# A second group of seven products in the last output projection of a two-layer decoder trunk

## The chip, the cores and the metric

One core of a Trainium2 chip runs the whole program in one launch. The metric is the device time of one execution in microseconds (us); lower is better. Engine names follow the profile: PE (TensorE matmul), PEld (its weight loads), DVE (VectorE), ACT (ScalarE), POOL (GpSimd), SP (SyncE, here only a queue that issues transfers).

## The reference, cut to what matters

Two layers work on 256 tokens of width 2048 in float32. Each layer normalises x, projects it, runs three token mixers a, b and c, projects each mixer's output to 2048 columns, and merges and projects once more:

```
g = jax.nn.sigmoid(gates).reshape(b, s, N_BRANCH, D_MODEL)
merged = g[:, :, 0] * y_a + g[:, :, 1] * y_b + g[:, :, 2] * y_c
return x + merged @ w_out
```

After the second layer a last RMSNorm gives the output. The change concerns `merged @ w_out` (256 x 2048 by 2048 x 2048) of the second layer and the order of the work just before it.

## The kernel before, in words

**Three products for one.** A float32 product is made of three on PE: every operand is split in a high part (a cast) and a low part (the rest), and high*high, low*high and high*low are summed in PSUM. The activations are split once. Weights stream from DRAM in blocks of 128 x 1024 words (512 KB); each block is cast on ACT (`high`, L296) and its rest taken on DVE (`low`, L300) just before use. There are three buffers each for the two parts.

**Steps.** `run` goes through a list of steps. A *plain* step has one weight block (256 rows by 512 columns): 12 matmuls of 128 x 512, for two token tiles, two row tiles and three products. In iteration s, `run` asks for the raw block of step s + 7, splits the block of step s + 2, and issues the matmuls of step s. Events hang on steps: work that is issued at a fixed distance from a step. The engines take their instructions in the order in which they were issued, so the list is the planner here, and each event's offset is a due time.

**Seven.** The class `Seven` is Winograd's form of Strassen's scheme on 1024 rows by 1024 columns (8 row tiles, two column blocks): products M1 to M7, two half steps each (`M1a`, `M1b`) of 6 matmuls, so 84 matmuls, where eight plain steps have 96. A half step still needs one whole block split. M1, M2 and M3 take raw blocks. The other four take sums of blocks, which are made in two pieces of memory for each half, `homes` and `third`: `two` and `three` load them on SP's queue, `first_sums` and `second_sum` add on DVE, and `first_adds` and `last_sum` add by transfers on POOL's queue that accumulate in memory. M5 and M3 take sums of activations (`osums`, made by `output_sums` from the merged tiles of column blocks 0 and 1). Results lie in four PSUM banks X, Y, Z, W; after M6 and M7 DVE forks a bank (L627: Z, then W). `lead` says how many steps before M5 the homes are asked for; `adds` says which sums are transfers.

**How the merged tile reaches the projection.** `merged` (called one step after the last product of column block j of branch b) multiplies and adds on DVE (L1612, L1613), and `turned` transposes: DVE transposes in blocks of 32 (L340), four POOL transfers write to DRAM (L343), one reads back (L349, `back`). Then `use_m` splits the result into `mx[j]`: a cast on ACT (L713), the rest on DVE (L714). `turned` puts its two later stages in a list of pending work: `back` at two plain steps' worth of work after the merge, `use_m` at `later` of them (`LATER` is 10). One entry is worked on at a time, in order. Both are issued `behind()`, that is, behind the splits of the step two ahead. `mx[2]` and `mx[3]` feed the second half of the rows of the output projection.

**The order before, last layer.** Gates `h1` (a group of seven and eight plain steps `c`, `d`) run beside `y1[0:8]`; then come `y1[8:16]` alone, four plain steps of output columns q = 2, then the group `o` (columns q = 0 and 1) interleaved with the four first steps of q = 3 and more of q = 2, then the last plain steps `c`, `e`, `f` (q = 2, 0, 1). The tail has the last four blocks of q = 3, the squares, the norm and the store. In the first layer the output projection already has two groups, `n` and `o` in the string `second`.

Of the kernel before, what the change touches and what calls it, by code (L numbers as in the profile page):

```python
# [11 lines left out]
ALU = mybir.AluOpType  # L12
# [77 lines left out]
def trunk(ctx: ExitStack, tc: tile.TileContext, x, w_in, xt, w_a, w_b, w_c, w_out,  # L90
# [115 lines left out]
    @contextmanager  # L206
    def in_turn():
        with tc.high_priority(offset=URGENT), issue_after(newest_parts[1].ins):
            yield
# [94 lines left out]
    def unit(*args, **kw):  # L304
        u = load_unit(*args, **kw)
        high(u)
        low(u)
        return u[1:]
# [42 lines left out]
    def turned(srcs, use, later=LATER, tmp=None, soon=False):  # L351


        n = len(srcs)
        if tmp is None:
            tmp = tp.tile([P, n * 512], F32, tag="zt", bufs=1, name=nm("zt"))
        c = srcs[0].shape[1]
        z = away([v.rearrange("p (k e) -> p k e", e=P) for v in srcs], tmp[:, :n * c], soon)

        def rest():  # L360
            y = tp.tile([P, n * 512], F32, tag="zy", bufs=1, name=nm("zy"))
            y = y[:, :n * c].rearrange("p (u k i) -> p u k i", u=n * 4, i=32)
            back(z, y)
            yield later - 2
            yield from use(y)

        pending.append([count[0] + 2, rest()])
# [115 lines left out]
    def once(make):  # L483
        kept = []

        def get():
            if not kept:
                kept.append(make())
            return kept[0]

        return get
# [8 lines left out]
    class Seven:  # L500


        def __init__(self, w, cols, act, sums, lead=7, own=None, adds=False, room=None, wide=False, copy_at=0):
# [29 lines left out]
            def three(h):  # L533
# [7 lines left out]
                with after_raw():  # L541
                    nc.sync.dma_start(third[h], block(1, 1, h))

            def first_adds(h):
                nc.gpsimd.dma_start(third[h], block(0, 1, h), accum_op=ALU.add)

            def first_sums(h):
                if own is not None:
                    with in_turn():
                        raw = self.steps["M1", h].raw  # L550
                        nc.vector.tensor_add(raw, raw, homes[h])
                    return
                with in_turn():
                    if adds in (1, 2, 4):
                        nc.vector.tensor_add(homes[h], homes[h], self.steps["M1", h].raw)
                        return
                    nc.vector.tensor_add(third[h], third[h], homes[h])
                    nc.vector.tensor_add(homes[h], homes[h], self.steps["M1", h].raw)

            def second_sum(h):  # L560
                if own is not None:
                    if adds:
                        nc.gpsimd.dma_start(homes[h], block(1, 1, h), accum_op=ALU.add)
                    with in_turn():
                        if not adds:
                            nc.vector.tensor_add(homes[h], homes[h], third[h])
                        nc.vector.tensor_add(third[h], third[h], self.steps["M1", h].raw)
                    return
                with in_turn():
                    nc.vector.tensor_add(homes[h], third[h], homes[h] if adds == 4 else self.steps["M1", h].raw)  # L570
                if adds == 4:
                    first_adds(h)

            def last_sum(h):
# [32 lines left out]
            for h in range(2):  # L607
                if lead:
                    st["M5", h].at(-PARTS - lead, partial(two, h), True)
                    st["M5", h].at(-PARTS - (lead + 1 if own is None else 3), partial(three, h), True)  # L610
                st["M1", h].at(-PARTS + (own is not None), partial(first_sums, h), True)
                if adds in (1, 2) and own is None:
                    st["M5", h].at(-PARTS - lead + 2, partial(first_adds, h), True)
                st["M5", h].at(-PARTS + 1, partial(second_sum, h), True)
                st["M2", h].at(-PARTS + 2, partial(last_sum, h), True)
            self.two, self.three = two, three
# [198 lines left out]
    for layer in range(DEPTH):  # L815
# [775 lines left out]
        def mg(j, t, mgs=mgs):  # L1591
            return mgs[j // 2][:, j % 2, t, :]
# [85 lines left out]
        def merged(b, j, y):  # L1678
            sg = held.pop((b, j), None)
            with in_turn() if b == 1 else nullcontext():  # L1680
                merge(b, j, y, sg)
            if b == 1:
                with in_turn():
                    turned([mg(j, t) for t in range(NT)], partial(use_m, j), LATER - 3 * (j in (1, 3) and not last), soon=True)

        kept_x, acc3 = {}, once(wide_accs)

        def output(q, banks, k0):
            if last and q == 3:
                return [plain(wo, k, q * 512, mx, acc3, k == 0, False) for k in range(0, KC, 2)]  # L1690

            def finished():
                xc = kept_x.pop(q)
                emit_x(xc, banks(), q, q * 512, list(range(NT)))
                store_x(xc, q * 512)

            def ask():
                kept_x[q] = residual(q * 512, 512)

            banks = once(banks or wide_accs)  # L1700
            steps = [plain(wo, k, q * 512, mx, banks, k == 0, k == KD - 2) for k in range(k0, KD, 2)]
            steps[-1].at(1, finished).at(-4, ask)
            return steps
# [52 lines left out]

        zg["M4", 1].at(1, partial(gate_summed, 0))
        zg["M3", 1].at(1, partial(gate_summed, 1))
        for i, st in enumerate((y1[2][3], f1[0]) if not last else y1[3][:2]):
            st.at(0, partial(output_sums, i * 2, i * 2 + 1))  # L1760
        if last:
            zd[3].at(0, lambda: nc.sync.dma_start(fwl[0], fnw.partition_broadcast(P)))
        if last:
            o = Seven(wo, (p0 * 512, p0 * 512 + 512), mx, osums, 10, None, 3)
            qs = {}
            for q in range(4):
                own = q in (p0, p0 + 1)
                banks = (lambda v: lambda: [o.bank(n) for n in v])("ZW" if q - p0 else "XY") if own else None
                qs[q] = output(q, banks, KC if own else 0)
        else:  # L1770
            c, d = 2 - p0, 3 - p0
            places = [once(lambda: slot().rearrange("p a b -> p (a b)")) for _ in range(2)]
            o = Seven(wo, (p0 * 512, p0 * 512 + 512), mx, osums, 10, None, 4, places, True)
            n = Seven(wo, (c * 512, d * 512), mx, osums, 9, None, 4, None, False, 5)
            qs = {q: output(q, lambda g=g, v=v: [g.bank(i) for i in v], KC)
                  for q, g, v in ((c, n, "XY"), (d, n, "ZW"), (p0, o, "XY"), (p0 + 1, o, "ZW"))}
# [14 lines left out]
        steps += gather(thin + rest, y=y2[10:], g=g1, c=c1, d=d1)  # L1791
        if last:
            steps += gather("y*2 " + begin.replace("M6a y", "M6a").replace("M2a y", "M2a") + rest, g=h1, y=y1[:8], c=e1, d=f1)
            steps += y1[8:]
        else:
            steps += gather("y*2 " + begin.replace("M6a y", "M6a").replace("M2a y", "M2a") +
                            "g.M3a c g.M3b c g.M4a c g.M4b c y*4", g=h1, y=y1[:12], c=e1)
# [10 lines left out]
        steps[at_norm].at(0, norm)  # L1808
        c, d = 2 - p0, 3 - p0
        if last:  # L1810
            steps += qs[c][:4] + gather(
                "g.M1a d g.M5a g.M1b d g.M5b d g.M6a d g.M6b c g.M2a c g.M2b g.M7a g.M7b g.M3a e g.M3b e g.M4a f g.M4b f c*2 e*2 f*2",
                g=o, c=qs[c][4:], d=qs[d], e=qs[p0], f=qs[p0 + 1])
        else:
            second = ("n.M1a h n.M1b h*3 y n.M5a y n.M5b y n.M6a n.M6b y n.M2a n.M2b n.M7a n.M7b "
                       "o.M1a c o.M1b d o.M5a c o.M5b d o.M6a n.M4a o.M6b n.M4b c*2 o.M2a d o.M2b o.M7a o.M7b n.M3a n.M3b d "
                       "o.M3a e o.M3b e o.M4a e o.M4b e f*4")
            steps += gather(second, n=n, o=o, y=y1[12:], h=f1, c=qs[c], d=qs[d], e=qs[p0], f=qs[p0 + 1])
# [15 lines left out]
            nc.vector.tensor_scalar(half, known, -0.5 / D, -0.5 * EPS, op0=ALU.mult, op1=ALU.add)  # L1834
            nc.vector.tensor_scalar(known, known, 1.0 / D, EPS, op0=ALU.mult, op1=ALU.add)

        c0, n = 1536, 512
        xc = residual(c0, n)

        head = acc3()  # L1840
        accs = [head[0], acc_tile()]
        nc.vector.tensor_add(xc[:, 1, :], head[1], xc[:, 1, :])
        oh, ol = ([slot(F32R).rearrange("p (k a) t -> p k (a t)", a=2) for _ in range(2)] for _ in range(2))
        for k0 in range(0, KC, 2):
            ks = slice(k0 % 4, k0 % 4 + 2)
            unit(w_out[layer], KC + k0, 2, [(c0, n)], dst=(oh[k0 // 4][:, ks, :], ol[k0 // 4][:, ks, :]))
        for t in range(NT):
            m, r, b = (small(1) for _ in range(3))
            kn, hf, ss = known[:, t:t + 1], half[:, t:t + 1], ssq[:, t, 3:4]
            if t < NT - 1:  # L1850
                for h in range(2):
                    token_products([accs[t]], n, (oh[h], ol[h]), mx, KC + h * 4, 4, KD, [t])
                emit_x(xc, [accs[t]], 3, c0, [t])
            else:

                token_products([accs[t]], n, (oh[0], ol[0]), mx, KC, 4, KD, [t], KC)
                token_products([accs[t]], n, (oh[1], ol[1]), mx, KC + 4, 2, KD - 2, [t], KC)
                with tc.high_priority(offset=URGENT):
                    nc.vector.tensor_add(xc[:, t, :], accs[t], xc[:, t, :])
                sa, kn, hf = (small(1) for _ in range(3))  # L1860
# [82 lines left out]
```

## Time and profile before

| what | value |
|---|---|
| three runs, median (lowest to highest) | 1976.4 us (1975.78 to 1977.06) |
| the profiled execution, its own time | 1976.76 us |
| its span, first to last instruction | 1974.7 us |
| PE busy | 1962.6 us (99%), 9158 matmuls |
| DVE busy | 1724.7 us (87%), 2022 instructions |
| ACT busy | 1357.5 us (69%), 1782 instructions |
| POOL busy | 234.2 us (12%), 354 instructions |
| granted TensorE clock, mean | 0.999 of full speed |

The span is what the instructions cover; the execution's own time has 2.06 us more around it. A busy share is an average over the whole span: an engine at 87% can be full for 20 us and half idle for the next 20.

### The profile page before, as it was taken

Reading aid. Unit: us, or ns where it says so; the run is one execution under the profiler, and the core shown is the slowest. Engines: PE = TensorE matmul, PEld = TensorE weight load, DVE = VectorE, ACT = ScalarE, POOL = GpSimd, SP = SyncE. Lnnn points to the kernel's source line nnn. Section 1 sums busy time; section 2 is a strip of 40 time slices with the busy share of each in tenths; the row PEclk is TensorE's granted clock in tenths of the full one; section 3 lists DMA queues with packets and bytes.
Section 4 is the critical chain, followed back from the end, with each engine's and each line's share of the span. In section 5 each row is a group of like instructions: output and inputs, shape, how many; then the busy total and the mean of one; then the engine's idle time right before and its main releaser. Section 6 shows DMA issues by size and latency. Waiting matters only on the chain.

```text
span 1974.7 us, 26272 instructions
## 1 busy us (share of the span) xinstructions
PE 1962.6 (99%) x9158; PEld 1642.7 (83%) x9158; DVE 1724.7 (87%) x2022; ACT 1357.5 (69%) x1782; POOL 234.2 (12%) x354
## 2 busy tenths in 40 slices
PE   9999999999999999999999999999999999999998
PEld 8888888888888888887888888888888888888886
DVE  8788999988998899889896988999889988898786
ACT  7567657679887666565665666676798876765654
POOL 0011102210100001012200211112101000011010
PEclk9999999999999999999999999999999999999999
DMA  7778759765888779889967787688659787798883
GB/s 276 279 253 270 238 188 315 266 226 190 257 265 268 235 243 297 268 288 322 331 232 277 250 270 233 199 294 280 218 180 290 246 285 249 242 294 270 288 279 136
DMA packets 147205, 507.86 MB, mean 257 GB/s; under 512 B 18368, under 2 KB 22976, under 8 KB 146944
## 3 DMA queue, kind: packets, MB, share of 16 engines
q1 hardware_dynamic: 116832, 409.18, 58.4%
q0 software_dynamic: 28576, 93.87, 19.0%
q10 hardware_dynamic: 1664, 3.15, 0.4%
q8 instruction: 71, 1.16, 0.2%
q14 instruction: 62, 0.51, 0.1%
HBM read 473.35 MB, written 32.77 MB: 256 GB/s over the span
## 4 chain that ended last, share of the span: by engine, by line
PE 98%; DVE 1%; issue 0%; DMA 0%; ACT 0%; DVEq 0%
PE acc L311 67%; PE mm L311 28%; PE mm L1313 1%; PE mm L1404 0%; PE mm L1455 0%; PE mm L1508 0%; PE mm L1371 0%; DVE wl L300 0%; PE mm L1485 0%; DMA raw<-in_w_in_dram 0%; PE mm L1284 0%; PE mm L1374 0%; PE mm L1513 0%; PE mm L1458 0%; DVE zt L340 0%
## 5 line engine op out<-in xcount | busy, mean ns | idle before, releaser
L311 PE MATMUL acc<-wh,s 128*128 128x512 f32 x3952 | 1007.8, 391 | 2.2 <-DVE s L714 1.1
L296 ACT CAST wh<-raw 128x1024 fp32r<-128x1024 f32 x636 | 663.4, 1046 | 376.7 <-PE acc L311 234.4
L300 DVE TENSOR_TENSOR wl<-raw,wh 128x1024 fp32r<-128x1024 f32 (+1 forms) x637 | 767.8, 1211 | 159.2 <-ACT wh L296 157.1
L311 PEld LDWEIGHTS acc<-wh,s 128*128 128x128 f32 x3952 | 734.7, 188 | 151.3 <-DVE acc L627 2.1
L311 PE MATMUL acc<-wl,s 128*128 128x512 f32 x1784 | 498.8, 390 | 0.1
L311 PEld LDWEIGHTS acc<-wl,s 128*128 128x128 f32 x1784 | 333.9, 188 | 71.2 <-DVE wl L300 2.0
L311 PE MATMUL mm<-wh,s 128*128 128x512 f32 (+1 forms) x1496 | 365.8, 385 | 0.0
L311 PEld LDWEIGHTS mm<-wh,s 128*128 128x128 f32 x1496 | 279.7, 188 | 54.6
L311 PE MATMUL mm<-wl,s 128*128 128x512 f32 (+1 forms) x748 | 198.2, 385 | 0.0
L343 POOL DMA_DIRECT2D z<-zt x192 | 113.8, 608 | 692.8 <-DVE zt L340 656.9
L311 PEld LDWEIGHTS mm<-wl,s 128*128 128x128 f32 x748 | 139.9, 188 | 27.0 <-DVE wl L300 0.4
L296 ACT CAST wh<-ar 128x1024 fp32r<-128x1024 f32 x92 | 96.9, 1053 | 71.7 <-PE acc L311 36.3
L300 DVE TENSOR_TENSOR wl<-ar,wh 128x1024 fp32r<-128x1024 f32 x92 | 111.7, 1219 | 15.2 <-ACT wh L296 14.3
L300 DVE TENSOR_TENSOR wl<-va,wh 128x1024 fp32r<-128x1024 f32 x52 | 63.5, 1220 | 18.0 <-ACT wh L296 17.7
L296 ACT CAST wh<-va 128x1024 fp32r<-128x1024 f32 x52 | 54.4, 1046 | 32.6 <-PE acc L311 13.7
L349 POOL DMA_DIRECT2D zy<-z x50 | 36.4, 729 | 300.0 <-DMA z<-zt 85.2
L311 PEld LDWEIGHTS mm<-s,wl 128*128 128x128 f32 x512 | 66.9, 191 | 5.0
L779 DVE SCALAR_TENSOR_TENSOR s<-yT,cst,s 128x256 f32<-128x256 f32 x160 | 69.2, 475 | 0.0
L311 PE MATMUL mm<-s,wl 128*128 128x192 f32 x512 | 66.0, 271 | 0.0
L774 ACT ACTIVATE zt<-yT,cst 128x256 f32<-128x256 f32 x128 | 57.5, 502 | 8.2 <-DVE s L1083 8.0
L774 ACT ACTIVATE ar<-yT,cst 128x256 f32<-128x256 f32 x136 | 60.3, 502 | 2.9 <-PE mm L1374 2.3
L774 ACT ACTIVATE s<-yT,cst 128x256 f32<-128x256 f32 x72 | 33.3, 521 | 30.2 <-DVE s L1083 30.1
(303 smaller groups left out, 1587.6 us busy)
## 6 DMA issues: line engine op xcount, KB each, us to landing
raw<-in_w_in_dram SPq DMA_DIRECT2D x497, 512.0 KB, 4.5
raw<-in_w_out_dram SPq DMA_DIRECT2D x49, 512.0 KB, 5.5
zy<-z POOLq DMA_DIRECT2D x48, 512.0 KB, 5.7
z<-zt POOLq DMA_DIRECT2D x184, 128.0 KB, 5.1
ar<-in_w_in_dram SPq DMA_DIRECT2D x28, 512.0 KB, 6.2
ar<-in_w_in_dram POOLq DMA_DIRECT2D x28, 512.0 KB, 8.4
raw<-in_w_a_dram SPq DMA_DIRECT2D x26, 512.0 KB, 6.5
raw<-in_w_b_dram SPq DMA_DIRECT2D x25, 512.0 KB, 4.2
```

The source lines that it names most:

```text
L296: newest_parts[0] = nc.scalar.copy(u[1], u[0])
L300: newest_parts[1] = sub = nc.vector.tensor_sub(u[2], u[0], u[1].bitcast(F32))
L311: newest[0] = nc.tensor.matmul(o, lhsT, rhs, start=start, stop=stop, skip_group_check=True)
L343: nc.gpsimd.dma_start(z[:, :, :, a, :].rearrange("t b c e -> c (t b) e"), tmp[a * 32:(a + 1) * 32].rearrange("c t b k i -> c (t b) (k i)"))
L349: nc.gpsimd.dma_start(y.rearrange("p (t a) k i -> p t (a k i)", a=4), z.rearrange("t b c a e -> (b c) t (a e)"))
L774: nc.scalar.activation(v, yT[:, c, q:q + S], AF.Identity if bias else AF.Copy, scale=wq, **b)
L779: nc.vector.scalar_tensor_tensor(o, yT[:, c, q:q + S], wq, o, op0=ALU.mult, op1=ALU.add)
L1313: nc.tensor.matmul(ps[:, q * S:(q + 1) * S], qi[i][:, hd, :], ki[j][:, 0, :], start=n == 0, stop=n == 2)
```

## The change

Only the second (last) layer's order is changed; the first layer's stays as it is.

- The first four steps of output columns q = 2 and q = 3 become a second group `n` on columns 1024 to 2047, with `lead` 14 and a new `adds` value, 6. Its four banks lie in two wide PSUM tiles; its homes are the fixed area `ar`, and `third` the buffers `ph` and `pl`. With `adds` 6 `first_sums` does nothing: a new function `plus` adds the block to its home by an accumulating transfer on POOL's queue, five steps after `two`. `second_sum` and `first_adds` are as with `adds` 4.
- The old group `o` gets `adds` 4 and two memory slots of its own for homes and third, and moves forward: it now runs interleaved with `y1[8:16]`, right after the gates. Then `n` runs, interleaved with the second halves of q = 0 and 1 (`e`, `f`) and of q = 2 (`c`).
- `output_sums` is asked for at the second and third of the gate steps `f1`, not at the fifth and sixth of `y1[8:16]`.
- In the last layer `use_m` is due after 7 plain steps' worth, not 10, for all four j.
- The tail takes its first sums of q = 3 from banks Z and W of `n`.

```
+            def plus(h):
+                nc.gpsimd.dma_start(homes[h], block(0, 0, h), accum_op=ALU.add)
+
...
                 with in_turn():
+                    if adds == 6:
+                        return
                     if adds in (1, 2, 4):
...
-                    nc.vector.tensor_add(homes[h], third[h], homes[h] if adds == 4 else self.steps["M1", h].raw)
-                if adds == 4:
+                    nc.vector.tensor_add(homes[h], third[h], homes[h] if adds in (4, 6) else self.steps["M1", h].raw)
+                if adds in (4, 6):
                     first_adds(h)
...
+                if adds == 6:
+                    st["M5", h].at(-PARTS - lead + 5, partial(plus, h), True)
...
-                    turned([mg(j, t) for t in range(NT)], partial(use_m, j), LATER - 3 * (j in (1, 3) and not last), soon=True)
+                    turned([mg(j, t) for t in range(NT)], partial(use_m, j), LATER - 3 * (last or j in (1, 3)), soon=True)
...
             if last and q == 3:
-                return [plain(wo, k, q * 512, mx, acc3, k == 0, False) for k in range(0, KC, 2)]
+                return []
...
-        for i, st in enumerate((y1[2][3], f1[0]) if not last else y1[3][:2]):
+        for i, st in enumerate((y1[2][3], f1[0]) if not last else (f1[1], f1[2])):
             st.at(0, partial(output_sums, i * 2, i * 2 + 1))
...
-            o = Seven(wo, (p0 * 512, p0 * 512 + 512), mx, osums, 10, None, 3)
...
+            places = [once(lambda: slot().rearrange("p a b -> p (a b)")) for _ in range(2)]
+            o = Seven(wo, (0, 512), mx, osums, 10, None, 4, places)
+            n = Seven(wo, (1024, 1536), mx, osums, 14, None, 6, None, True)
+            qs = {q: output(q, lambda g=g, v=v: [g.bank(i) for i in v], KC)
+                  for q, g, v in ((0, o, "XY"), (1, o, "ZW"), (2, n, "XY"), (3, n, "ZW"))}
...
-            steps += y1[8:]
...
-            steps += qs[c][:4] + gather(
-                "g.M1a d g.M5a g.M1b d g.M5b d g.M6a d g.M6b c g.M2a c g.M2b g.M7a g.M7b g.M3a e g.M3b e g.M4a f g.M4b f c*2 e*2 f*2",
-                g=o, c=qs[c][4:], d=qs[d], e=qs[p0], f=qs[p0 + 1])
+            steps += gather("o.M1a y o.M1b y o.M5a y o.M5b y o.M6a y o.M6b y o.M2a y o.M2b y o.M7a o.M7b "
+                            "o.M3a o.M3b e*2 o.M4a f o.M4b f n.M1a n.M1b n.M5a e n.M5b e n.M6a f n.M6b f "
+                            "n.M2a n.M2b n.M7a n.M7b n.M3a c n.M3b c n.M4a c n.M4b c",
+                            n=n, o=o, y=y1[8:], c=qs[2], e=qs[0], f=qs[1])
...
-        head = acc3()
+        head = [n.bank("Z"), n.bank("W")]
```

## Rows read from the trace of the kernel before

**Rows 1.** Page, parts 1 and 4: engines' busy time, and the chain that ended last.
```profile
PE 1962.6 (99%) x9158; PEld 1642.7 (83%) x9158; DVE 1724.7 (87%) x2022; ACT 1357.5 (69%) x1782; POOL 234.2 (12%) x354
...
PE 98%; DVE 1%; issue 0%; DMA 0%; ACT 0%; DVEq 0%
```
**Rows 2.** Windows: span, busy us of PE, PEld, DVE, ACT, POOL; clock, DMA share, GB/s.
```profile
1840.00:1860.00 20.00, 20.00 (x90) 16.57 (x89) 11.88 (x10) 10.95 (x13) 1.11 (x2) 1.00 0.77 260
1860.00:1880.00 20.00, 20.00 (x90) 16.57 (x89) 18.84 (x25) 12.21 (x15) 2.33 (x4) 1.00 0.91 325
```
**Rows 3.** Page, part 5: the splits of weight blocks; busy us, mean ns, idle before.
```profile
L296 ACT CAST wh<-raw 128x1024 fp32r<-128x1024 f32 x636 | 663.4, 1046 | 376.7 <-PE acc L311 234.4
L300 DVE TENSOR_TENSOR wl<-raw,wh 128x1024 fp32r<-128x1024 f32 (+1 forms) x637 | 767.8, 1211 | 159.2 <-ACT wh L296 157.1
```
**Rows 4.** Timeline of PE, last layer: start, length, instruction, count.
```profile
1830.94 1.07 PE L311 MATMUL acc<-wh,s 128*128 128x512 f32 x4
...
1889.56 1.98 PE L311 MATMUL mm<-wh,s 128*128 128x512 f32 x8
...
1892.29 1.07 PE L311 MATMUL acc<-wh,s 128*128 128x512 f32 x4
...
1893.64 1.98 PE L311 MATMUL mm<-wh,s 128*128 128x512 f32 x8
...
1899.09 1.98 PE L311 MATMUL mm<-wh,s 128*128 128x512 f32 x8
...
1922.22 1.07 PE L311 MATMUL acc<-wh,s 128*128 128x512 f32 x4
...
1960.30 5.67 PE L311 MATMUL acc<-s,s 128*128 128x512 f32 x30
```
**Rows 5.** Timeline of DVE, last layer.
```profile
1861.17 1.22 DVE L714 TENSOR_TENSOR s<-zy,s 128x1024 fp32r<-128x1024 f32 x1
...
1869.60 1.28 DVE L714 TENSOR_TENSOR s<-s,s 128x512 fp32r<-128x512 f32 x2
...
1872.09 1.22 DVE L1612 TENSOR_TENSOR t<-mm,t 128x1024 f32<-128x1024 f32 x1
1873.34 1.23 DVE L1613 TENSOR_TENSOR s<-s,t 128x1024 f32<-128x1024 f32 x1
...
1875.62 1.30 DVE L340 STREAM_TRANSPOSE zt<-s 128x512 f32<-128x512 f32 x2
...
1905.20 1.22 DVE L714 TENSOR_TENSOR s<-zy,s 128x1024 fp32r<-128x1024 f32 x1
...
1922.83 0.69 DVE L627 TENSOR_TENSOR acc<-ev,acc 128x512 f32<-128x512 f32 x1
...
1924.57 1.22 DVE L714 TENSOR_TENSOR s<-zy,s 128x1024 fp32r<-128x1024 f32 x1
```
**Rows 6.** Timeline of POOL, last layer: reads of turned tiles, with what each waited for.
```profile
1829.59 0.71 POOL L349 DMA_DIRECT2D zy<-z  x1 [7.63 <-DMA z<-zt]
...
1885.39 0.72 POOL L349 DMA_DIRECT2D zy<-z  x1 [5.85 <-DMA z<-zt]
```
**Rows 7.** Timeline of PE, first layer's two groups: the two places where PE waited.
```profile
898.18 0.73 PE L311 MATMUL acc<-wh,s 128*128 128x512 f32 x2 [1.06 <-DVE s L714]
...
919.86 1.20 PE L311 MATMUL acc<-wh,s 128*128 128x512 f32 x4 [0.96 <-DVE acc L627]
```
**Rows 8.** Timeline of DVE, first layer's two groups.
```profile
875.34 1.23 DVE L714 TENSOR_TENSOR s<-zy,s 128x1024 fp32r<-128x1024 f32 x1 [1.71 <-ACT s L713]
...
897.45 1.28 DVE L714 TENSOR_TENSOR s<-s,s 128x512 fp32r<-128x512 f32 x2
```
**Rows 9.** Timeline of ACT, first layer's two groups.
```profile
874.26 1.05 ACT L713 CAST s<-zy 128x1024 fp32r<-128x1024 f32 x1 [1.88 <-DMA zy<-z]
```
**Rows 10.** DMA issues: count, KB each, median us from issue to landing.
```profile
zy<-z POOLq DMA_DIRECT2D x48, 512.0 KB, 5.7
...
ar<-in_w_out_dram POOLq DMA_DIRECT2D x4, 512.0 KB, 11.9
```

More of the change, by code (lines that the diff above doesn't have):

```diff
@@ L1683, in merged @@
                 with in_turn():
-                    turned([mg(j, t) for t in range(NT)], partial(use_m, j), LATER - 3 * (j in (1, 3) and not last), soon=True)
-        kept_x, acc3 = {}, once(wide_accs)
+                    turned([mg(j, t) for t in range(NT)], partial(use_m, j), LATER - 3 * (last or j in (1, 3)), soon=True)
+        kept_x = {}
         def output(q, banks, k0):
             if last and q == 3:
-                return [plain(wo, k, q * 512, mx, acc3, k == 0, False) for k in range(0, KC, 2)]
+                return []
             def finished():
@@ L1763, in trunk @@
         if last:
-            o = Seven(wo, (p0 * 512, p0 * 512 + 512), mx, osums, 10, None, 3)
[L1765 to L1769, printed above, removed]
+            places = [once(lambda: slot().rearrange("p a b -> p (a b)")) for _ in range(2)]
[3 more added lines that the diff above has]
+                  for q, g, v in ((0, o, "XY"), (1, o, "ZW"), (2, n, "XY"), (3, n, "ZW"))}
         else:
@@ L1835, in trunk @@
             nc.vector.tensor_scalar(known, known, 1.0 / D, EPS, op0=ALU.mult, op1=ALU.add)
-        c0, n = 1536, 512
-        xc = residual(c0, n)
-        head = acc3()
+        c0, width = 1536, 512
+        xc = residual(c0, width)
+        head = [n.bank("Z"), n.bank("W")]
         accs = [head[0], acc_tile()]
@@ L1845, in trunk @@
             ks = slice(k0 % 4, k0 % 4 + 2)
-            unit(w_out[layer], KC + k0, 2, [(c0, n)], dst=(oh[k0 // 4][:, ks, :], ol[k0 // 4][:, ks, :]))
+            unit(w_out[layer], KC + k0, 2, [(c0, width)], dst=(oh[k0 // 4][:, ks, :], ol[k0 // 4][:, ks, :]))
         for t in range(NT):
@@ L1851, in trunk @@
                 for h in range(2):
-                    token_products([accs[t]], n, (oh[h], ol[h]), mx, KC + h * 4, 4, KD, [t])
+                    token_products([accs[t]], width, (oh[h], ol[h]), mx, KC + h * 4, 4, KD, [t])
                 emit_x(xc, [accs[t]], 3, c0, [t])
             else:
-                token_products([accs[t]], n, (oh[0], ol[0]), mx, KC, 4, KD, [t], KC)
-                token_products([accs[t]], n, (oh[1], ol[1]), mx, KC + 4, 2, KD - 2, [t], KC)
+                token_products([accs[t]], width, (oh[0], ol[0]), mx, KC, 4, KD, [t], KC)
+                token_products([accs[t]], width, (oh[1], ol[1]), mx, KC + 4, 2, KD - 2, [t], KC)
                 with tc.high_priority(offset=URGENT):
```

## The prediction

> **What bounds the kernel now.** I read the busy times first, then the chain of waits, the windows of the last 130 us, and the engines' timelines there. PE is busy 99% of the span and makes 98% of the chain that ended last [rows 1]: the time falls by the matmuls that go, and rises by every microsecond that PE newly waits. So the question is whether DVE, ACT and the transfers can still hide. The whole-span share of DVE, 87%, says little: in one 20 us window it is busy 11.88 us, in the next 18.84 us, with PE full in both [rows 2]. What hides today hides in such unequal stretches. The other thing to see is the first layer, whose output projection already has two groups of seven: PE waits twice there, 1.06 us for the low part of activation sums and 0.96 us for a fork [rows 7]. Together they are 2.0 us, the nearest measured price for what the last layer now gets.
>
> **What goes.** A plain step takes 1892.29 - 1889.56 = 2.73 us, a half step 1893.64 - 1892.29 = 1.35 us [rows 4]. Eight plain steps (96 matmuls) become fourteen half steps (84): one plain step less, -2.73 us of PE. Nothing else leaves PE, and the tail's last 5.67 us of matmuls [rows 4] and the norm behind them stay.
>
> **What is added for DVE and ACT.** Fourteen blocks are split in place of eight: six more, about 6.3 us of ACT (1046 ns each) and 7.3 us of DVE (1211 ns) [rows 3]. The vector sums don't grow: six in the old group before; now four in `o` and two in `n`, since `plus` takes two. From `o.M1a` to the end of the list there are 34 steps' worth, 92.8 us. DVE has to do in them: 48 splits, 58; six sums at about the 1.22 of a block-sized instruction, 7; four forks at 0.69, 3; two merges at 1.22 + 1.23 + 1.30, 7.5; two `use_m` subtractions, 2.4; three ends of a column block (four half-size instructions each, at the fork's 0.69), 8 [rows 3, 5]. That is some 86 of 92.8 us: it fits on the average, so these cost nothing by themselves, and I look for places where they bunch.
>
> **First place: `e0`, the first step that reads mx[2].** The merge of j = 2 hangs on `o.M6a`; 7.5 steps' worth later its `use_m` comes due at `o.M3b`, and `e0` is the very next step. It needs the high part at its start, 1.35 us after the due step began, and the low part one third into itself, 0.91 us later: 2.26 us in all. Before, the same instruction ended 3.57 us after its due step began when DVE was idle now and then (1922.22 to 1924.57 + 1.22), and 7.33 us when DVE was full (1899.09 to 1905.20 + 1.22) [rows 4, 5]; nothing waited, as the reader was steps away. So PE waits between 1.3 and 5.1 us. By the queue: the merge of j = 3 lands on `o.M7a`, in front. Back to back, DVE starts an instruction every 1.14 us (1873.34 to 1875.62 with one split between [rows 5]). From 0.4 us after `o.M7a` begins it has the splits of M3a, M3b, `e0`, `e1` and the L714 (5.7), the merge (2.3), its transposes (1.2) and the fork (0.6): done at 10.2 us. `e0` wants it at four half steps + 0.91 = 6.3 us: 3.9 us late, or 1.5 if the transposes and L1613 let it pass. I take 3.2, nearer the first, since transposes are asked for at higher priority. ACT's cast and the split behind it then wait too, but on a PE that waits anyway.
>
> **Second place: the activation sums at `o.M5a`.** `use_m` of j = 1 is now due 6 steps after M7b of `h1` (1830.94 [rows 4]) ends, at about 1848.7 on the clock of before; its L714 should start near 1853. M5a wants the low part of the sums at 1868.3 (seven steps' worth after 1848.7, and a third): 15.3 us. Before, L714 to the last low part of the sums took 1861.17 to 1870.88, 9.7 us, among plain steps alone [rows 5]; in the first layer, among half steps, sums and merges, 875.34 to 898.73, 23.4 us [rows 8], and PE waited 1.06 us [rows 7]. Of the 9.7 some 4.1 were splits of 3.6 steps. In the new stretch DVE has L714, six splits, three weight sums (10 x 1.14 = 11.4) and that 5.6: 17.0 us for 15.3. So 0 to 1.7; I take 1.0, the first layer's price.
>
> **Smaller ones.** `use_m` of j = 0 is due at 1830.94, but its read was issued at 1829.59 [rows 6] and lands 5.7 us later [rows 10], at 1835.3. If ACT already stands at that cast, the split for `g.M3b` ends about 1837.4 for a step that starts at 1836.4: 0 to 2.0 us with the second copy; I take 0.2, as a cast that waited 1.88 us in the first layer [rows 9] cost PE nothing. `use_m` of j = 3 is due at `n.M1b`, read by `e2` 3.6 us later; against 3.57 to 7.33 that is 0 to 3.7; DVE's queue there (splits of M5a and `e2`, one sum, L714, 4.6 us) says 0.4 beyond cover, which I take. The fork behind `n.M7b` has one half step of cover, as the one of 0.96 us had [rows 7]: 0 to 0.96, taken 0.1. `plus` costs DVE nothing and is asked 6.5 steps (17.7 us) before its reader, against 11.9 us for such a transfer to land [rows 10]; if it came late, each microsecond would hold M5a's split on ACT. On POOL and SP the six accumulating and four plain transfers of the new group, and the two more of the old, take queue time while PE runs: 0.
>
> **The sum.** -2.73 + 3.2 + 1.0 + 0.2 + 0.4 + 0.1 = +2.2 us. The profiled execution took 1976.76 us, its span 1974.70 and 2.06 around it; with +2.2 it is 1978.9. It stood 0.36 above the median of the runs, so I predict **1978.6 us**. With all low ends it would be 1975.0, with all high ends 1987, which no one stretch can pay, as a PE that waits in one place lets DVE catch up for the next.
>
> [...] A cast of ACT waited 1.88 us for a transfer and the splits behind it stood still [rows 9]. [...] The read of a turned tile, 512 KB, landed in 5.7 us, an accumulating one in 11.9 [rows 10]. [...]
>
> **The rivals.**
> - *The covers hold.* L714 passes the transposes, and the sums of activations end in time. For it: PE waited only twice in the denser first layer, 2.0 us in all [rows 7]. Against: there no reader stood right behind its due step. Waits of at most 1.4 us: 1973.7 to 1975.1, about 1974.5.
> - *Slower: DVE becomes the bound at `o.M5a`.* The weight sums and merges go ahead of the activation sums, as in the first layer. Price: their time less 15.3 us. At 20 us PE waits 4.7 instead of 1.0: 1982.3; at the first layer's 23.4 [rows 8] it is 1985.7. It decides the sign of a measurable change from about 18 us on. Against: PE paid only 1.06 there.
> - *Late transfers.* The chain of j = 2 from merge to landing took 1872.09 to 1885.39 + 5.7, 19.0 us [rows 5, 6]; it now has some 19.3 to its due step (20.5 from `o.M6a` to `o.M3b`, the merge starting some 1.2 in). More traffic could add 3 to 6 us, and the part beyond DVE's own lateness falls on `e0`: 1980 to 1984. Here belongs also that the change does not do what it says: that slots for homes or `plus` come late, and the sums are waited for after all.
>
> **How the numbers follow.** Forecast 0.50, covers hold 0.22, DVE at M5a 0.20, late transfers 0.08. A measurement tells about 0.2%, 4.0 us, from no change. No case reaches -4.0, as PE loses only 2.73 us of work: faster 0.02, for what I have not seen. Slower: 0.17 + 0.05 of the two late cases and 0.03 of the forecast, 0.25. Same: 0.73. The range 1974.3 to 1983.0 holds the forecast's own 1976.5 to 1981, more than half of the covers' case and the nearer half of the late ones. The forecast sits inside "same", yet above the old median.
>
> **What would show it.** Right: 12 matmuls fewer on PE; a PE wait of 1.5 to 4 us in `e0` put down to DVE's L714, one of about 1 us in `o.M5a`; DVE without a gap from `o.M7a` to `e0`; six weight sums on DVE, as before, and ten accumulating transfers of weight blocks on POOL where it had two. Wrong: no gap in front of `e0` (covers hold), a gap over 3 us at `o.M5a`, or PE waiting on ACT's L713 or on a raw block.

## The result, and the profile after

The changed kernel took 1997.75 us (median of 4 runs, 1997.26 to 1998.42) against 1976.56 before (4 runs), a ratio of 1.0108 [1.0092, 1.0123]: 21 us slower, where the forecast was 2 and the range ended at 1983.0. The profiled execution has a span of 1995.5 us, 20.8 more than before. In this file `L713` and `L714` have become L720 and L721, L627 is L634, and `plus` is L545.

The page, parts 1, 4 and 5, against [rows 1, 3]:
```profile
PE 1964.7 (98%) x9146; PEld 1641.6 (82%) x9146; DVE 1732.6 (87%) x2031; ACT 1364.2 (68%) x1790; POOL 242.0 (12%) x362
...
PE 3%; DVE 0%; ACT 0%; issue 0%; DVEq 0%
...
L311 PE MATMUL acc<-wh,s 128*128 128x512 f32 x3952 | 1010.8, 391 | 18.6 <-ACT s L720 13.6
```
The 12 matmuls are gone (9158 to 9146). The chain no longer reaches back to the start: it could be followed only to a wait of PE at 1918.25 us. The last row says which wait to look for: 13.6 us in which PE stood until a cast of ACT (L720) was done. The prediction had named a PE that waits for this cast as a sign of being wrong.

The timeline of PE in the last layer, where it waited, and the groups behind the long wait (start, length, instruction, count, idle before):
```profile
1858.07 2.11 PE L311 MATMUL acc<-wh,s 128*128 128x512 f32 x8 [1.25 <-ACT wh L296]
...
1866.93 0.73 PE L311 MATMUL acc<-wl,s 128*128 128x512 f32 x2 [0.71 <-DVE wl L300]
...
1871.61 0.73 PE L311 MATMUL acc<-wh,s 128*128 128x512 f32 x2 [0.76 <-DVE s L721]
...
1914.95 2.08 PE L311 MATMUL acc<-wh,s 128*128 128x512 f32 x4 [13.57 <-ACT s L720]
1918.29 2.08 PE L311 MATMUL acc<-wh,s 128*128 128x512 f32 x4 [1.27 <-DVE s L721]
1920.16 1.91 PE L311 MATMUL acc<-wl,s 128*128 128x512 f32 x4
1921.87 2.48 PE L311 MATMUL acc<-wh,s 128*128 128x512 f32 x8
1924.19 1.09 PE L311 MATMUL acc<-wl,s 128*128 128x512 f32 x4
1925.12 1.07 PE L311 MATMUL acc<-wh,s 128*128 128x512 f32 x4
...
1959.53 1.17 PE L311 MATMUL mm<-wh,s 128*128 128x512 f32 x4 [1.48 <-DVE mm L634]
```
These are six waits, 19.04 us in all, 14.84 of them in the step `e0`. The kernel before has no wait of PE in this stretch. A second loss stands in the lengths: four matmuls take 2.08 us behind the long wait and 1.07 later. From 1914.95 to 1925.12 the two steps `e0` and `e1` take 10.17 us; two usual steps and the wait of 1.27 are 6.72, so 3.45 us went on a slower clock (granted 0.50 from 1906 to 1922 us, 1.00 again from 1924). The sum -2.73 + 19.04 + 3.45 is 19.8 of the 20.8 us; 1.0 is not explained.

POOL's timeline shows why the tile of j = 2 came late, and ACT's and SP's (its queue's own) the two ends of it:
```profile
1887.30 2.41 POOL L343 DMA_DIRECT2D z<-zt  x4 [5.09 <-DVE zt L340]
1897.66 0.96 POOL L545 DMA_DIRECT2D ar<-in_w_out_dram  x1 [7.95 <-DMA ar<-in_w_out_dram]
1902.77 0.88 POOL L545 DMA_DIRECT2D ar<-in_w_out_dram  x1 [4.15 <-DMA ar<-in_w_out_dram]
1903.39 1.01 POOL L349 DMA_DIRECT2D zy<-z  x1
```
```profile
1855.08 1.05 ACT L720 CAST s<-zy 128x1024 fp32r<-128x1024 f32 x1 [6.24 <-DMA zy<-z]
...
1913.85 1.04 ACT L720 CAST s<-zy 128x1024 fp32r<-128x1024 f32 x1 [11.78 <-DMA zy<-z]
```
```profile
1883.78 0.40 SPq L531 DMA_DIRECT2D ar<-in_w_out_dram  x1
...
1888.97 0.44 SPq L531 DMA_DIRECT2D ar<-in_w_out_dram  x1
```
The homes `ar` were asked for at 1883.78 and 1888.97 and `plus` could start at 1897.66 and 1902.77, 13.9 and 13.8 us later. POOL stood before each of them, and behind both stood the read of the turned tile (L349, no wait of its own). The cast of ACT that waited for it could start at 1913.85, and `e0` started 1.1 us later. In the kernel before, nothing stood between the writes and the read at 1885.39 [rows 6], which followed them by 8.2 us; here it is 16.1 us. The writes of before:
```profile
1877.22 2.33 POOL L343 DMA_DIRECT2D z<-zt  x4 [31.53 <-DVE zt L340]
```

Two views of the transfers: windows (as in [rows 2]), and then the issues between 1880 and 1910 us (count, KB each, median us to landing):
```profile
1880.00:1900.00 20.00, 20.00 (x90) 16.57 (x89) 17.17 (x17) 10.55 (x10) 4.22 (x6) 1.00 1.04 334
...
1910.00:1920.00 10.00, 3.79 (x8) 2.59 (x9) 2.36 (x2) 1.99 (x2) 0.73 (x1) 0.50 0.84 329
```
```profile
raw<-in_w_out_dram SPq DMA_DIRECT2D x7, 512.0 KB, 15.0
ar<-in_w_out_dram SPq DMA_DIRECT2D x2, 512.0 KB, 13.3
...
zy<-z POOLq DMA_DIRECT2D x1, 512.0 KB, 10.4
```
The transfer engines are full (share 1.04), and the median raw block needs 15.0 us to land. The same view of the kernel before has 4.8 us:
```profile
raw<-in_w_out_dram SPq DMA_DIRECT2D x8, 512.0 KB, 4.8
```
The granted clock of 1910 to 1920 us is 0.50, where that of 1880 to 1900 is 1.00; PE had stood for 13.57 us until 1914.95, and while it stood, the window 1900 to 1910 already had 0.79.

### The profile page after: what moved, and what is told of

It reads as the page before. It is cut to its first block, busy times and chain, and to the rows that moved or that the text cites. A ratio compares the mean times of both kernels' runs of the same rounds, so it can differ in the third digit from the quotient of the medians.

```text
span 1995.5 us, 26297 instructions
## 1 busy us (share of the span) xinstructions
PE 1964.7 (98%) x9146; PEld 1641.6 (82%) x9146; DVE 1732.6 (87%) x2031; ACT 1364.2 (68%) x1790; POOL 242.0 (12%) x362
## 5 line engine op out<-in xcount | busy, mean ns | idle before, releaser
L311 PE MATMUL acc<-wh,s 128*128 128x512 f32 x3952 | 1010.8, 391 | 18.6 <-ACT s L720 13.6
L349 POOL DMA_DIRECT2D zy<-z x50 | 36.8, 736 | 311.5 <-DMA z<-zt 95.3
L300 DVE TENSOR_TENSOR wl<-s,wh 128x1024 fp32r<-128x1024 f32 x36 | 43.8, 1217 | 17.8 <-ACT wh L296 17.5
```

The source lines that it names most:

```text
L300: newest_parts[1] = sub = nc.vector.tensor_sub(u[2], u[0], u[1].bitcast(F32))
L311: newest[0] = nc.tensor.matmul(o, lhsT, rhs, start=start, stop=stop, skip_group_check=True)
L349: nc.gpsimd.dma_start(y.rearrange("p (t a) k i -> p t (a k i)", a=4), z.rearrange("t b c a e -> (b c) t (a e)"))
```

## The experiments

Twelve kernels ran in four groups (`e1` to `e4`, `e5` to `e8`, `e9` and `e10`, `e11` and `e12`), each with the kernel before on the same chip (medians 1978.14, 1978.12, 1977.65 and 1978.02 us). A ratio below is against that median. `e1` to `e12` are names of runs here; where a step of the list is meant, the text says the step `e0` or the step `e1`.

**1. Queue or load.** In `e1` the new group's first sums are made by DVE, and `plus` goes:
```diff
-            n = Seven(wo, (1024, 1536), mx, osums, 14, None, 6, None, True)
+            n = Seven(wo, (1024, 1536), mx, osums, 14, None, 4, None, True)
```


> The changed kernel with its new group's first sums made by the vector engine, as in the old group: no accumulating transfer stands on POOL's queue between the writes and the read of the turned tile of column block 2. Theory Q (the read was queued behind two accumulating transfers that waited for their homes, 1889.7 to 1903.4 us): the read is issued when the writes have landed, about 1895.5, lands by 1902, PE's wait in e0 falls from 13.57 + 1.27 to some 4 us, the clock stays up, and the time is 1981 to 1985 us. Rival T (the transfer engines are full from 1876 to 1906, so the read would have landed late anyway): the read takes 10 us, PE waits some 8, 1987 to 1991. Rival D (the reader stands too close behind its due step, my forecast): 3 to 5 us of PE wait stay in e0 under either.

In `e2`, `plus` stays and may go only behind the last read of a turned tile:
```diff
+                with issue_after(last_back[0].ins):
+                    nc.gpsimd.dma_start(homes[h], block(0, 0, h), accum_op=ALU.add)
```


> The changed kernel with one issue order added: the two accumulating transfers of the new group stand behind the read of column block 2 on POOL's queue. Theory Q: as with the vector sums, within 1.5 us (1981 to 1985); the transfers, some 6 to 10 us later, still land before M5a's split needs them. Rival T: no better than 1987. If the accumulating transfers themselves are the load that slows the read, this and the vector sums agree; if it is the homes' plain loads, both stay slow.

In `e3` the homes are asked for 20 places ahead in place of 14:
```diff
-            n = Seven(wo, (1024, 1536), mx, osums, 14, None, 6, None, True)
+            n = Seven(wo, (1024, 1536), mx, osums, 20, None, 6, None, True)
```


> The changed kernel with the new group's homes asked for six steps sooner still (lead 20 for 14), so also its accumulating transfers. Theory Q: homes have landed when the accumulating transfers come up, they finish before the writes of block 2 are issued, the read is issued near 1895.5, and the time is 1981 to 1985. Rival T: the same bytes move to a stretch where the engines have room (60 to 230 GB/s at 1872 to 1876), so the read lands in under 7 us; if only Q counts, it lands as in the run with vector sums. If the order alone mattered and not the wait for the homes, the read stays behind them and nothing changes (1997).

Measured: `e1` 1988.8 us, 1.0057 [1.004, 1.0074]; `e2` 1989.15, 1.0059 [1.0044, 1.0074]; `e3` 1998.45, 1.0104 [1.0089, 1.0119]. POOL's timeline of `e1`, then of `e3`:
```profile
1888.43 2.40 POOL L343 DMA_DIRECT2D z<-zt  x4 [5.09 <-DVE zt L340]
1897.82 0.71 POOL L349 DMA_DIRECT2D zy<-z  x1 [6.99 <-DMA z<-zt]
```
```profile
1897.14 0.86 POOL L545 DMA_DIRECT2D ar<-in_w_out_dram  x1 [11.25 <-DMA ar<-in_w_out_dram]
1897.68 2.71 POOL L343 DMA_DIRECT2D z<-zt  x4
1909.01 0.72 POOL L349 DMA_DIRECT2D zy<-z  x1 [8.62 <-DMA z<-zt]
```
POOL's timeline of `e2`, where L351 is the read and L548 is `plus`:
```profile
1892.18 2.40 POOL L343 DMA_DIRECT2D z<-zt  x4 [5.08 <-DVE zt L340]
1901.04 0.71 POOL L351 DMA_DIRECT2D zy<-z  x1 [6.46 <-DMA z<-zt]
1902.40 0.95 POOL L548 DMA_DIRECT2D ar<-in_w_out_dram  x1 [0.65 <-DMA ar<-in_w_out_dram]
```
With `plus` away or behind the read, the read goes 9.4 us (`e1`) and 8.9 us (`e2`) after the writes, and some 9 us of time come back (some 10 when each kernel is held against its own median of before), with the same accumulating transfers still made in `e2`. So they are lost by the place in POOL's queue and not by the work of `plus`. `e3` moved the harm: the first `plus` went early, but the second home, asked for at 1881.49, landed 15.7 us later, and `plus` stood 11.25 us for it, now in front of the writes of the same tile. Asking six places sooner did not help, as the second landing took longer still.

What stays in `e1` is 10.7 us. PE's timeline of `e1`, the two waits in the step `e0`:
```profile
1906.23 2.07 PE L311 MATMUL acc<-wh,s 128*128 128x512 f32 x4 [3.71 <-ACT s L720]
1909.57 2.08 PE L311 MATMUL acc<-wh,s 128*128 128x512 f32 x4 [1.27 <-DVE s L721]
```

**2. The reader behind its due step.** `e4` is `e1` with the readers of mx[2] moved four half steps back:
```diff
-                            "o.M3a o.M3b e*2 o.M4a f o.M4b f n.M1a n.M1b n.M5a e n.M5b e n.M6a f n.M6b f "
+                            "o.M3a o.M3b o.M4a o.M4b n.M1a n.M1b e*2 f*2 n.M5a e n.M5b e n.M6a f n.M6b f "
```


> The changed kernel with vector sums in the new group, and its order changed: M4 of the old group and M1 of the new one go between M3b and e0, so that the first reader of block 2 comes 2 plain steps' worth (5.4 us) after its due step. Rival D: against the run with vector sums the wait of 3 to 5 us in e0 goes, 1978 to 1981. Theory T: some 3 us of wait stay, as the read lands late. Left in all: the waits of 0.7 to 1.5 us at the fifth-last gate step, o.M1b, o.M5a and the last fork, 4.2 us together.

Measured: 1990.72 us, 1.0064 [1.0049, 1.0079], no gain over `e1`. ACT's timeline of `e4` says why:
```profile
1904.53 1.05 ACT L720 CAST s<-zy 128x1024 fp32r<-128x1024 f32 x1 [3.05 <-DMA zy<-z]
1905.48 1.04 ACT L296 CAST wh<-raw 128x1024 fp32r<-128x1024 f32 x1
```
The reader went back, but the cast did not. It is asked for 7 steps after the merge, when the tile has not landed yet, and the splits of whatever step comes next stand behind it on ACT: PE waited 3.05 us, now for `wh`, the high part of a weight block.

**3. The parts alone.** `e5` is the kernel before with only the shorter due time:
```diff
-                    turned([mg(j, t) for t in range(NT)], partial(use_m, j), LATER - 3 * (j in (1, 3) and not last), soon=True)
+                    turned([mg(j, t) for t in range(NT)], partial(use_m, j), LATER - 3 * (last or j in (1, 3)), soon=True)
```


> The kernel before with one edit of the change: the turned tiles of j = 0 and j = 2 are due 7 steps after their merge instead of 10; order of steps, groups and transfers as before. Theory: due sooner costs only where the read is still under way when ACT reaches the cast, and where a reader stands close behind; before, the reads landed 5.7 us after their issue and the readers are many steps away, so 1976 to 1979 us, with ACT's cast waiting 0 to 4 us and PE at most about 1 us. Rival (the shorter due time alone costs much, since a cast that waits on ACT holds the splits behind it): 1981 to 1985.

The edit shortens the due time of all four tiles, not of j = 0 and 2 alone.

`e6` adds to `e5` the old group's new place, and has no second group (columns 1024 to 2047 are plain steps):
```diff
+            o = Seven(wo, (p0 * 512, p0 * 512 + 512), mx, osums, 10, None, 4, places)
...
+            steps += gather("o.M1a y o.M1b y o.M5a y o.M5b y o.M6a y o.M6b y o.M2a y o.M2b y o.M7a o.M7b "
+                            "o.M3a o.M3b e*2 o.M4a f o.M4b f c d e c d e c d f c d f c*4",
```


> The change without its second group: the old group runs among the last eight steps of y, with its own places, four accumulating transfers and the due time of 7, and its first two reader steps stand where the changed kernel has them; columns 1024 to 2047 stay plain steps, 12 in place of 14 half steps of the new group and the four behind it, so PE has the 2.73 us back. Theory (what is left of the loss with the new first sums on VectorE, 10.7 us, comes from the transfers of the new group, which fall into the same stretch as the writes and reads of the turned tiles): the read of j = 2 lands within about 8 us, e0 waits 0 to 3 us, 1978 to 1982 us. Rival (it comes from moving the old group and its reader forward): the waits of the run with sums on VectorE stay, 1986 to 1991.

`e7` is `e4` with two steps of `y` ahead of the old group, so that ten half steps, from `o.M2a` to `n.M1b`, stand without a plain one between them:
```diff
+            steps += gather("y*2 o.M1a y o.M1b y o.M5a y o.M5b y o.M6a y o.M6b y o.M2a o.M2b o.M7a o.M7b "
+                            "o.M3a o.M3b o.M4a o.M4b n.M1a n.M1b e*2 f*2 n.M5a e n.M5b e n.M6a f n.M6b f "
```


> The change with the new group's first sums on VectorE, two of the eight steps of y ahead of the old group (so that the merge of j = 2 falls behind the fourth step of y two half steps sooner against the group), and the readers of mx[2] moved from behind o.M3b to behind n.M1b: from merge to first reader there is 4.5 steps more cover less what the shorter interleave takes. Theory (what is left is a read that lands too late for its reader, and a cast on ACT that waits for it): the wait at e0 falls to 0 to 2 us, the sums of the activations at o.M5a get 2.7 us more, and the time is 1979 to 1984. Rival (the stretch as a whole lacks transfer or VectorE time, and a wait moved away comes back elsewhere): 1986 to 1991, with waits among the half steps of o that now stand without plain steps between them.

`e8` is `e1` without the last layer's eight accumulating transfers (`first_adds` and `last_sum` of both groups), so its weight sums lack their last terms. The diff shows `last_sum`:
```diff
+                if adds == 5:
+                    return
                 if adds > 1:
                     nc.gpsimd.dma_start((homes if own is None else third)[h], block(1, 0, h), accum_op=ALU.add)
```


> The change with the new group's first sums on VectorE and without the eight accumulating transfers of the two groups of the last layer: the last terms of their weight sums are left out, so that the output lacks them; nothing else moves. Theory (full transfer engines between 1876 and 1906 us hold the landing of the read of j = 2 and of the raw blocks): the share of the engines there falls from 0.99 by a third of it, the read lands in 5 to 7 us instead of 7.3, e0's wait falls below 2 us, 1977 to 1983. Rival (due time and VectorE's queue set the waits, whatever the transfers do): within 2 us of the run with them, 1987 to 1991.

Measured: `e5` 1981.84 us, 1.0022 [1.0011, 1.0034]; `e6` 1989.1, 1.0054 [1.0039, 1.0069]; `e7` 1985.65, 1.0038 [1.0026, 1.0051]; `e8` 1989.27, 1.0054 [1.0039, 1.0069]. Three rows of `e5`, from the timelines of ACT, DVE and PE:
```profile
1896.41 1.05 ACT L713 CAST s<-zy 128x1024 fp32r<-128x1024 f32 x1 [3.34 <-DMA zy<-z]
...
1897.49 1.22 DVE L714 TENSOR_TENSOR s<-zy,s 128x1024 fp32r<-128x1024 f32 x1 [2.07 <-ACT s L713]
...
1904.45 1.04 PE L311 MATMUL acc<-wl,s 128*128 128x512 f32 x2 [2.05 <-DVE wl L300]
```
The cast stands for 3.34 us, DVE idles 2.07 with the weight sums still to make, ACT then waits 3.06 for one of them, and PE 2.05 for the splits behind it. From 1904.45 to 1908.89 it runs 12 matmuls in 4.44 us where 2.73 is usual (granted clock 0.83 from 1900 to 1910 us): 2.05 + 1.7 = 3.75 us. The median lies 3.7 us above that of before, but this profiled execution, at 1983.81, lies 5.7 above it, so 2 us of it are not explained here. The expectation fell between its theories: no reader stands close, and yet the shorter due time costs, through DVE's queue.

`e6` refutes its theory. It has no new group, has as many matmuls as the kernel before, and is as slow as `e1`. PE's timeline of `e6`:
```profile
1860.39 2.12 PE L311 MATMUL acc<-wh,s 128*128 128x512 f32 x8 [2.14 <-ACT wh L296]
...
1869.25 0.74 PE L311 MATMUL acc<-wl,s 128*128 128x512 f32 x2 [0.69 <-DVE wl L300]
...
1873.92 0.73 PE L311 MATMUL acc<-wh,s 128*128 128x512 f32 x2 [0.71 <-DVE s L714]
...
1906.07 1.80 PE L311 MATMUL acc<-wh,s 128*128 128x512 f32 x4 [2.38 <-ACT s L713]
1909.47 2.07 PE L311 MATMUL acc<-wh,s 128*128 128x512 f32 x4 [1.61 <-DVE s L714]
```
The waits are 7.53 us; the steps `e0` and `e1` take 9.80 us from 1906.07 to 1915.87 where two steps and 1.61 are 7.07, so 2.7 more for the clock (granted 0.82 from 1900 to 1910 us, 0.84 from 1910 to 1920): 10.3 of 11.0. Most of what was left of the loss in `e1` comes with the old group moved forward, with its near reader and near due times. Most and not all, as `e1` has 2.73 us less of matmuls: it loses 10.7 + 2.73 = 13.4 us elsewhere and `e6` 11.0, so the second group gives back nearly all that it saves.

`e8` speaks against the load as its cause as well. The share of the transfer engines in 1880 to 1900 us falls from 1.04 to 0.81 (it is still 1.01 from 1900 to 1910), the read lands in 6.0 us instead of 7.3 (issue to cast), and the time stays. The raw blocks issued from 1880 to 1910 us, in `e1` and then in `e8`:
```profile
raw<-in_w_out_dram SPq DMA_DIRECT2D x8, 512.0 KB, 12.6
```
```profile
raw<-in_w_out_dram SPq DMA_DIRECT2D x8, 512.0 KB, 5.2
```
The waits in the step `e0` are 1.62 and 2.96. The second is DVE's queue: L723, the low part, runs at 1909.38, and from the fork at 1904.19 on DVE has no gap in front of it.

`e7` met neither theory: the waits at 1858 to 1872 us are gone, the step `e0` waits 1.89 instead of 4.98, and 4.16 us turn up among the ten half steps, for a split behind ACT's cast, which stands 5.14 us for the tile.

**4. The cast later.** `e9` is `e7` with the cast of j = 2 two steps later (and that of j = 3 one step sooner):
```diff
-                    turned([mg(j, t) for t in range(NT)], partial(use_m, j), LATER - 3 * (last or j in (1, 3)), soon=True)
+                    turned([mg(j, t) for t in range(NT)], partial(use_m, j), LATER - ((3, 3, 1, 4)[j] if last else 3 * (j in (1, 3))), soon=True)
```


> The run with two steps of y ahead and the reader moved back, with one more edit: the turned tile of j = 2 is due 9 steps after its merge instead of 7 (that of j = 3 is 6 instead of 7 after its own, which is the same place in the list, since its read stands behind the use of j = 2). Theory (ACT came to the cast 5.14 us before the read of j = 2 had landed, and stood there with the splits behind it): the cast comes 5.4 us later and finds the tile there; the waits of 4.16, 0.68 and 1.21 us shrink to at most 1.5 in all, the low clock behind them goes, and 1976 to 1980 us come out. Rival (VectorE and the raw blocks cannot feed the ten half steps of o that stand alone): PE still waits 3 us or more there, 1982 to 1986.

`e10` also puts a plain step behind `n.M7b`:
```diff
-                            "o.M3a o.M3b o.M4a o.M4b n.M1a n.M1b e*2 f*2 n.M5a e n.M5b e n.M6a f n.M6b f "
-                            "n.M2a n.M2b n.M7a n.M7b n.M3a c n.M3b c n.M4a c n.M4b c",
+                            "o.M3a o.M3b o.M4a o.M4b n.M1a n.M1b e*2 f*2 n.M5a e n.M5b e n.M6a f n.M6b "
+                            "n.M2a n.M2b n.M7a n.M7b f n.M3a c n.M3b c n.M4a c n.M4b c",
```


> The same with the last step of the second column block moved behind n.M7b, so that a plain step, which has its own accumulators, covers the fork that held the next step for 1.48 us: 1.5 us less than the run without this move if the fork was only late by its own length, 1974.5 to 1978.5 us if that run comes out as its theory says. Rival: the fork is asked for only when VectorE reaches it behind other work, or what follows the wait was slack anyway, and the time is within 0.7 us of the run without the move.

`e11` is `e6` with the near reader moved away, and j = 2 due at 10 as before:
```diff
-                            "o.M3a o.M3b e*2 o.M4a f o.M4b f c d e c d e c d f c d f c*4",
+                            "o.M3a c o.M3b d o.M4a c o.M4b d c d c d e*2 f*2 e*2 f*2 c*4",
```


> The run with the old group forward and columns 1024 to 2047 as plain steps, with two edits: the steps that read mx[2] stand behind the plain steps of the other columns, eight steps later, and the turned tile of j = 2 is due 10 steps after its merge, as in the kernel before; the tiles of j = 0, 1 and 3 stay at 7. Theory (of the 11.0 us of that run, the wait in front of the near reader and the low clock behind it are some 6 to 7; the rest, 3.5 us of waits at the sums for o.M1a to o.M5a, is the near due time of j = 1): the waits of 2.38 and 1.61 us go, those of 2.14, 0.69 and 0.71 stay, 1980 to 1983.5. Rival (half steps among the last eight steps of y cost this much whatever stands behind them): 1986 to 1990.

`e12` is `e9` with the new group's blocks asked for later:
```diff
-            n = Seven(wo, (1024, 1536), mx, osums, 14, None, 4, None, True)
+            n = Seven(wo, (1024, 1536), mx, osums, 9, None, 4, None, True)
```


> The run in which the tile of j = 2 is due 9 steps after its merge, with the new group's homes and third blocks asked for 9 places ahead of n.M5 instead of 14. Theory (there the wait has become one for blocks: ACT waits 1.32 and 2.51 us for an accumulated sum and a raw block while the engines of the transfers are full from 1880 to 1910 us): four blocks of 512 KB leave the start of that stretch, the landings of raw blocks get shorter, the waits of ACT for blocks fall below 1.5 us in all and PE's 2.37 us with them, 1978.5 to 1982 us. Rival (the blocks are wanted inside the stretch anyway, so that a later request only moves the queue): within 1.5 us of the run with 14 places, 1982.5 to 1986, with the wait at the first sums of n instead.

Measured: `e9` 1983.9 us, 1.0035 [1.0023, 1.0047]; `e10` 1984.35, 1.0037 [1.0024, 1.0049]; `e11` 1980.89, 1.0017 [1.0008, 1.0027]; `e12` 1989.21, 1.0054 [1.0037, 1.0071]. PE's timeline of `e11`, all its waits in the last layer:
```profile
1860.77 2.11 PE L311 MATMUL acc<-wh,s 128*128 128x512 f32 x8 [1.43 <-ACT wh L296]
...
1869.64 0.73 PE L311 MATMUL acc<-wl,s 128*128 128x512 f32 x2 [0.67 <-DVE wl L300]
...
1874.32 0.73 PE L311 MATMUL acc<-wh,s 128*128 128x512 f32 x2 [0.76 <-DVE s L714]
```
As its theory said, both waits of the step `e0` and the slow clock behind them go (granted 1.00 from 1900 to 1920 us), 8 of the 11 us, and 2.86 us of waits at j = 1 stay. The median is 2.9 us above that of before; that the two agree is in part chance, as this profiled execution (1983.09) lies 5.1 above. The run moved the reader and the due time of j = 2 together, and no run parts the two. ACT's timelines of `e9` and then DVE's of `e12` show the next limit:
```profile
1901.03 1.04 ACT L296 CAST wh<-raw 128x1024 fp32r<-128x1024 f32 x1 [2.51 <-DMA raw<-in_w_out_dram]
```
```profile
1910.23 1.23 DVE L560 TENSOR_TENSOR ar<-ar,va 128x1024 f32<-128x1024 f32 x1 [5.34 <-DMA ar<-in_w_out_dram]
```
In `e9` the cast no longer waits; a split waits for its raw block instead, and PE 2.37 us with it. The half steps without plain steps between them want blocks at twice the rate of plain ones (one in 1.35 us, not in 2.73), and the transfer engines are full (share 1.03 to 1.04 from 1880 to 1910 us). Asking for the homes later (`e12`) makes it worse than either theory had: DVE waits 5.34 us for a home, and PE 5.59. The rival had the place right, but not the size. `e10` gains nothing: the wait of 1.48 us behind `n.M7b` is gone, but where the plain step was taken from, behind `n.M6b`, the fork there now costs this (PE's timeline of `e10`):
```profile
1938.16 1.15 PE L311 MATMUL mm<-wh,s 128*128 128x512 f32 x4 [0.95 <-DVE mm L634]
```
A wait among the ten half steps is 0.55 us longer too (2.92 against 2.37), and that makes up the rest.

No version here beats the kernel before. At most 2.73 us, 0.14%, is to be won. The nearest, `e11`, has no second group of seven and so could not win it.

## Why the prediction was wrong

**The step that failed** is in "Smaller ones": "`plus` costs DVE nothing and is asked 6.5 steps (17.7 us) before its reader", and after it "On POOL and SP the six accumulating and four plain transfers of the new group, and the two more of the old, take queue time while PE runs: 0." I held `plus` against its own reader, and never looked who stands behind it on POOL while it waits for its home. It was the read of j = 2, whose chain I had measured at 19.0 us against 19.3 to its due step, so it had 0.3 us of slack. In place of that 0 the runs showed a read that left 7.9 us later behind its writes than in the kernel before, and 9 to 10 us of time (`e1`, `e2`). Even the sum of all high ends, 1987, lay nearly 11 us below the result: a term was missing, and not only sizes off.

The trace shows the order on POOL: the read, with no wait of its own, stood behind both `plus`, which waited 7.95 and 4.15 us, and went 0.62 us after the second. I had counted such a hold for ACT alone, where a cast had waited 1.88 us [rows 9].

**The clock** was in no term: 3.45 us behind the wait at the step `e0` (granted 0.50), and 1.7 to 2.7 in `e5` and `e6` (0.83 and 0.82 from 1900 to 1910 us). The range counted waits only, so it was too narrow even where the waits were right.

**The landing times.** I priced reads at 5.7 us and accumulating transfers at 11.9, the medians of a whole run [rows 10]. In this stretch raw blocks took 15.0 us, homes 13.3 and the read 10.4. The homes' landing had no price at all.

**The step `e0`, the first place:** the place was right, the mechanism right in part, and the size too small. With `plus` away the wait is 4.98 us (`e1`), 3.99 (`e6`) and 4.58 (`e8`), where I took 3.2 of 1.3 to 5.1. One part is DVE's queue as drawn: in `e6` the low part ended 11.3 us after `o.M7a` began at 1898.09, where I had 10.2, and DVE had no gap before it:
```profile
1908.20 1.22 DVE L714 TENSOR_TENSOR s<-zy,s 128x1024 fp32r<-128x1024 f32 x1
```
The other part is ACT's cast, which stood for the read (2.00 us in `e6`); I had counted that as free. `e11` shows the whole as the price of the near reader and the near due time together.

**`o.M5a`:** 0.76 measured, 1.0 taken. DVE was full there (19.76 of 20 us from 1860 to 1880), but the 4.7 us and more of that rival did not come. My 17.0 us of DVE work counted L714 twice, as the 5.6 in it begin with it; 15.9 is right, and DVE took 15.4 (1856.16 to 1871.56). The list of 86 us of DVE work left out the other 4.5 of these 5.6 us; with them it is 90 of 92.8, which still fits on the average.

**j = 1** was missing. I looked at the read of j = 0 (no wait of PE) and let j = 1's L714 "start near 1853". Its read went out at 1846.43 us, the cast stood 6.24 us for it, and L714 started at 1856.16. The cast held a split, for which PE waited 1.25 us at 1858.07. DVE, which had stood 6.06 us for the cast, then had no gap, and PE waited 0.71 for a split of it at 1866.93. With two plain steps more ahead (`e7`) both waits are gone.

**j = 3 and the step `e2`:** no wait, 0.4 taken. **The fork behind `n.M7b`:** 1.48 us against 0 to 0.96. It has no cover at all: in the new group the half step behind it writes the other half of the same wide accumulator tile, and so waits for the whole fork; `e10`, with a plain step there, does not wait. `n.M7b` ended at 1958.05 us, and DVE was at a split:
```profile
1957.56 1.22 DVE L300 TENSOR_TENSOR wl<-va,wh 128x1024 fp32r<-128x1024 f32 x1
1958.69 0.69 DVE L634 TENSOR_TENSOR mm<-ev,mm 128x512 f32<-128x512 f32 x1
```
The rest of that split, the fork and 0.14 us make the 1.48.

**The matmuls:** -2.73 us, right.

The rival of late transfers named the right place, with a chance of 0.08 and 1980 to 1984 us. It had the landing late by 3 to 6 us and no queue. For the 9 to 10 us it is the order in which POOL issues the transfers that counts (`e1`, `e2`), and taking accumulating transfers away did not win back the rest (`e8`).

## What to carry to other kernels

On POOL a transfer that waited for another one held what stood behind it until that had landed (7.95 and 4.15 us here). For each transfer that is added, write down what stands behind it on the same queue, and hold its start against the slack of what stands there. A tile's due time is a place in ACT's and DVE's queues: a due time ahead of the landing stopped what stood behind it even with no reader near (`e5`, 3.34 us of ACT and 2.05 of PE). Half steps save matmuls and double the rate of blocks and splits (one in 1.35 us here, not in 2.73); between them plain steps are the cover. With the second group in place, moving the reader (`e4`) or the homes (`e12`) won nothing.

## What the runs showed of the hardware that was not expected

A wait of PE can cost more than itself. Behind 13.57 us of wait the next 24 matmuls took 3.45 us more (groups of four 2.08 us instead of 1.07); in `e5` 12 matmuls took 1.7 us more behind a wait of 2.05. It is not the length of the wait alone: behind 2.14 us at 1860.39 in `e6`, eight matmuls took 2.12 us, near the usual 1.98. The granted clock was 0.83 from 1900 to 1910 us in `e5` and stayed at 1.00 from 1840 to 1880 in `e6`. What tells the two cases apart no run here shows.

The same plain transfer of 512 KB had no fixed landing time. Raw blocks issued between 1880 and 1910 us landed in 4.8 us in the kernel before, 15.0 in the changed one, 12.6 in `e1` and 5.2 in `e8` (medians). The share of the transfer engines from 1880 to 1900 us was 0.82, 1.04, 1.04 and 0.81.
